# Head chunks and token sums: two chunks per store, stored by GpSimd, loaded by a gather of the feature block

## The chip, the cores and the metric

The kernel runs on one core of a Trainium2 chip. A core has five engines that work side by side, each through its own queue of instructions in order: TensorE (PE; its weight loads are shown apart as PEld), VectorE (DVE), ScalarE (ACT), GpSimd (POOL) and SyncE (SP, which here does nothing but issue transfers). Transfers between the core's memory and the chip's main memory (DMAs) are issued by SP, ACT or POOL and carried out by 16 DMA engines. The metric is the device time of one execution in microseconds (us), lower is better.

## The reference, cut to what matters

Two layers of a backbone over 1024 tokens of width 1024: a retention layer (4 heads, queries and keys of 256, values of 512, chunks of 128 tokens), a SwiGLU FFN, a short gated convolution, and a second FFN. What the change touches is the way from the heads to the o projection, and operands of the FFNs' and the convolution's last products:

```python
def retention_output(o, g, w_o):
    bsz, nh, L, dv = o.shape
    o = o * lax.rsqrt(jnp.mean(o * o, axis=-1, keepdims=True) + EPS)
    o = o.transpose(0, 2, 1, 3).reshape(bsz, L, nh * dv).astype(g.dtype)
    return (jax.nn.silu(g) * o) @ w_o
...
        hx = hx + g1 * yx
        fx = modulate(rms_norm(hx, norm_ffn[i]), sh2, sc2)
        hx = hx + g2 * swiglu(fx, ffn_w1[i], ffn_w3[i], ffn_w2[i])
```

Here `o` is each head's retention output, `g` the gate and `w_o` a matrix of 2048 by 1024. All is fp32.

## The kernel before

**Products.** Every fp32 product is made of three passes of a split type (`mm3`, L130 low part of one operand, L131 of the other, L132 both high parts). The operands come from `split`: ACT casts the high part (L125), DVE subtracts it for the low part (L126). The large projections do seven products of half matrices in place of eight, so they need sums and differences of operands: n = 1 to 7 names the product. The operands that several products share are written to main memory by whoever makes them and loaded again by the projection.

**The retention phase** (up to about 890 us) goes through the heads one after the other and, in each, through chunks in both directions. `read` (L730) multiplies queries with the state and with the chunk's values, `update` renews the state (L723 and L724 make its high and low parts on ACT and DVE). L672 (ACT) and L673 (POOL) split the values. At the end of a head, each chunk c of eight goes through `finish` (L766): DVE multiplies it by the gate that `gate` has loaded (L763, L769), PE transposes it in four pieces (L774) into one bank, ACT copies it out (L776) to a tile `og` of 128 partitions by 512, which is four feature blocks of 128 by the 128 tokens of the chunk. `store` (L780) writes it from ACT to `og_d`, whose layout is [partition, feature block, 512 tokens]: one chunk goes to four pieces of 512 bytes in each partition. Then `o_finish` runs what the chunk before has left in `o_late`: the sums over tokens that the o projection's seven products need, `first` (head 1 minus head 0, L811) and `others` (three, L816, L818 and L820, when the second head of a pair is in its second half of tokens), each stored to `os_d` in the same way. In all 24 stores to `og_d` and 32 to `os_d`, 256 KB each, by ACT.

**The o projection** follows in the same instruction streams: its first operands are made while the last head ends. `down` (L1120) runs the products in the order n = 1, 5, 6, 3, 7, 4, 2, each with eight steps of 12 matmuls; for each step it loads an operand tile from `og_d` or `os_d` (`x_loads`, L1145; a whole feature block, 512 tokens, in one piece of 2 KB in each partition), up to three ahead, and pieces of `w_o` (`w_load`, L1132), makes the sums of weights (L1159, L1161) and splits both. `load_h` (L1173) loads the residual from `in_xT`. `o_src` says which tile a step reads. The FFNs and the convolution use the same `down` with operands from `x_d`: `x_steps` makes them and `put` stores them from ACT (182 stores, L1267).

**What sets the order.** The kernel is written as steps that are queued, and a scheduler of the framework fixes the order of instructions on each engine when the program is built. Transfers that SP and ACT issue are given eight landing counters (DMAHW0 to DMAHW7 in the listings below) in turn; a transfer waits, in its engine's queue, until the one before on its counter has landed. POOL's transfers have eight counters of their own (DMASW0 to DMASW7). An engine stands still while the instruction at the head of its queue waits.

Of the kernel before, what the change touches and what calls it, by code (L numbers as in the profile page):

```python
# [17 lines left out]
P = 128  # L18
# [33 lines left out]
def hybrid_kernel(ctx: ExitStack, tc: tile.TileContext, a: dict):  # L52
    nc = tc.nc
# [14 lines left out]
    def raw():  # L68

        return up.tile([P, 1024], F32, tag="u", name="raw")  # L70
# [450 lines left out]
    og_d = spilled("og_d", HEADS, NTB, shape=(P, 4, 512))  # L521
    os_d = spilled("os_d", 4, HEADS // 2, shape=(P, 4, 512))
    x_d = spilled("x_d", 7, FT // 2)
# [47 lines left out]
    for kt, h in enumerate(ch):  # L571
        if kt % 2 == 0:
            x = unit()
# [68 lines left out]
    vs, qh, kh, sh, st, s_hl, part, loaded, gates = {}, {}, {}, {}, {}, {}, {}, {}, {}  # L642
# [123 lines left out]
    def finish(h, c):  # L766

        gt = gates[h, c]
        nc.vector.scalar_tensor_tensor(  # L769
            gt, part[h, c], ys[h][:, c : c + 1], gt, op0=ALU.mult, op1=ALU.mult  # L770
        )
        ot = bank()
        for b in range(4):
            nc.tensor.transpose(ot[:, b * P : (b + 1) * P], gt[:, b * P : (b + 1) * P], ident)  # L774
        og, put = o_place(h, c)
        nc.scalar.copy(og, ot)  # L776
        t = slice((c % 4) * P, (c % 4 + 1) * P)

        def store(dst, src):
            nc.scalar.dma_start(dst[:, :, t], src.rearrange("p (b t) -> p b t", b=4))  # L780

        if (h % 2, c // 4) != (0, 1):
            store(og_d[h][c // 4], og)
        o_finish()
        if put is not None:
            o_late.append(lambda: put(store))
        gate(h, c + G_AHEAD)


# [1 line left out]
    o_parts, o_late = {}, []  # L791
# [5 lines left out]

    def o_place(h, c):

        p, i, j, c4 = h // 2, h % 2, c // 4, c % 4  # L800
        if (i, j) == (1, 1):
            og = ttile()
        else:
            if c4 % 2 == 0:
                o_parts[p, "r"] = raw()
            og = o_parts[p, "r"][:, (c4 % 2) * 512 : (c4 % 2 + 1) * 512]
            o_parts[p, i, j, c4] = og

        def first(store):
            x11 = o_parts[p, 0, 0, c4]  # L810
            nc.vector.tensor_sub(x11, og, x11)  # L811
            store(os_d[0][p], x11)

        def others(store):
            t1, x12, x21 = (o_parts.pop((p, *k, c4)) for k in ((0, 0), (0, 1), (1, 0)))
            nc.vector.tensor_sub(t1, og, t1)  # L816
            store(os_d[1][p], t1)
            nc.vector.tensor_sub(x12, og, x12)  # L818
            store(os_d[2][p], x12)
            nc.vector.tensor_sub(x21, x21, t1)  # L820
            store(os_d[3][p], x21)

        return og, {(0, 1): first, (1, 1): others}.get((i, j))

    seq = [(None, [(0, n) for n in range(NCX)])]
# [292 lines left out]
    def down(src, nh, w, gate, residual, order, consume, then=(), last=False):  # L1120
# [15 lines left out]
        def x_loads(end, must=False):  # L1136

            while loaded[0] < min(end, len(seq)):
                m = loaded[0]
                if src(*seq[m]) is None:  # L1140
                    if not must:
                        return
                    until(lambda: src(*seq[m]) is not None)
                xl[m] = ttile()
                nc.sync.dma_start(xl[m], src(*seq[m]))  # L1145
                loaded[0] += 1

        def operands(m):
# [112 lines left out]
    def x_steps(n_pairs):  # L1261


        parts, have = {}, set()

        def put(n, pr, t):
            nc.scalar.dma_start(x_d[n - 1][pr], t)  # L1267
            have.add((n, pr))

        def take(pr, i, j, t):  # L1270
            parts[pr, i, j] = t
            if (i, j) != (0, 1):
                put({(0, 0): 1, (1, 0): 2, (1, 1): 3}[i, j], pr, t)
            if all((pr, i, j) in parts for i in range(2) for j in range(2)):
                x11, x12, x21, x22 = (parts.pop((pr, i, j)) for i in range(2) for j in range(2))

                t2, t4 = [], []

                def one():
                    nc.vector.tensor_sub(x12, x12, x11)  # L1280
                    put(5, pr, x12)
                    t2.append(ttile2())
                    nc.vector.tensor_sub(t2[0], x22, x12)
                    put(6, pr, t2[0])

                def two():
                    nc.vector.tensor_sub(x11, t2[0], x11)
                    put(7, pr, x11)
                    t4.append(ttile2())
                    nc.vector.tensor_sub(t4[0], x21, t2[0])  # L1290
                    put(4, pr, t4[0])

                hooks.extend([nothing] * (4 if pr == 0 else 0) + [one, two])

        return take, lambda n, pr: x_d[n - 1][pr] if (n, pr) in have else None
# [131 lines left out]
    def o_src(n, i):  # L1427
        p, b = i // 4, i % 4
        k, tb = S_X.get(n, (0 if n == 5 else 1, 0))
        if 2 * p + k not in o_ready:  # L1430
            return None
        src = og_d[2 * p + k][tb] if n in S_X else os_d[{5: 0, 6: 1, 7: 2, 4: 3}[n]][p]
        return src[:, b]

    fx, w_plain = {}, {}
    o_ahead, o_run = down(
# [4 lines left out]
    for i, (r, _) in enumerate(seq):  # L1441
# [8 lines left out]
        if r is not None and r[1] == steps - 1:  # L1450
            h = r[0]
# [195 lines left out]
```

## Time and profile before

| what | value |
|---|---|
| median of 3 runs | 2657.06 us (2656.66 to 2660.74) |
| the profiled execution | 2653.21 us, its span 2651.4 us |
| PE busy | 2580.5 us, 97% of the span |
| DVE busy | 1944.9 us, 73% |
| ACT busy | 1191.6 us, 45% |
| POOL busy | 124.5 us, 5% |
| mean granted PE clock | 0.989 |

The span runs from the first to the last instruction of the profiled execution; the device time holds it and what lies around it. Busy time counts arithmetic only, and not the issuing of transfers; the names ACTq and SPq stand for such issues. A row of a timeline gives its start, its length, the engine, the line of the kernel, the operation with output and inputs, its shape and, in brackets, how long the engine stood idle before it and what it had waited for. The granted clock says at which share of full speed PE was allowed to run.

### The profile page before, as it was taken

To read this page: it belongs to the slowest core of one execution; us is meant where nothing else is said; L and a number is where in the kernel's file an instruction comes from. 1 tells how busy PE (TensorE), PEld (TensorE's weight loads), DVE (VectorE), ACT (ScalarE), POOL (GpSimd) and SP (SyncE) were. 2 spreads that over 40 slices of the span, in tenths; PEclk is the share of its full clock that TensorE was granted. 3 is DMA by queue.
4 is the path that set the end of the run, shared out by engine and by line. 5 is a ranking of instruction groups with operands and counts; after the bars stand their busy time and mean duration, and the time that the engine had idled before them with its cause. 6 is when DMAs were issued, how large, how long until landed. Compare 5 with 4: busy or idle time off the path is not lost.

```text
span 2651.4 us, 32772 instructions
## 1 busy us (share of the span) xinstructions
PE 2580.5 (97%) x11448; PEld 2108.8 (80%) x11448; DVE 1944.9 (73%) x3404; ACT 1191.6 (45%) x2162; POOL 124.5 (5%) x92
## 2 busy tenths in 40 slices
PE   8999999999989799999999999999999999999998
PEld 4788888887777587888888888888777888888886
DVE  4876776767887768877776878777798666567874
ACT  4743333447866436433333446433355333334452
POOL 1100221002210000000000000000000000000000
PEclk9999999999999899999999999999999999999999
DMA  9556234763668742445546734122552233328532
GB/s 330 196 166 220 83 116 151 247 226 120 201 205 270 226 126 88 147 144 178 190 152 205 267 99 155 39 81 96 177 200 72 96 109 106 111 92 300 172 100 84
DMA packets 216069, 420.43 MB, mean 159 GB/s; under 512 B 21984, under 2 KB 51808, under 8 KB 215904
## 3 DMA queue, kind: packets, MB, share of 16 engines
q1 hardware_dynamic: 134640, 310.53, 36.9%
q10 hardware_dynamic: 81264, 107.81, 11.3%
q8 instruction: 90, 1.47, 0.2%
q14 instruction: 75, 0.61, 0.1%
HBM read 308.68 MB, written 109.58 MB: 158 GB/s over the span
## 4 chain that ended last, share of the span: by engine, by line
PE 87%; DVE 5%; DMA 4%; issue 2%; ACT 1%; ACTq 0%; POOL 0%; SPq 0%; DVEq 0%; POOLq 0%
PE ps L130 28%; PE ps L131 28%; PE ps L132 28%; DVE u L126 1%; PE ps L993 1%; DVE u L724 1%; DMA og_d<-tt 0%; DVE kh L683 0%; DMA tt<-x_d 0%; DMA raw<-in_xT 0%; DMA raw<-in_w_kc 0%; PE ps L289 0%; DMA tt<-in_cxT 0%; ACT u L125 0%; PE ps L774 0%
## 5 line engine op out<-in xcount | busy, mean ns | idle before, releaser
L130 PE MATMUL ps<-u 128*128 128x512 f32 x3472 | 1364.0, 394 | 28.8 <-DVE u L126 17.0
L131 PE MATMUL ps<-u 128*128 128x512 f32 x3472 | 1360.2, 392 | 1.2 <-DVE u L126 1.2
L132 PE MATMUL ps<-u 128*128 128x512 f32 x3472 | 1357.3, 391 | 0.0
L130 PEld LDWEIGHTS ps<-u 128*128 128x128 f32 x3472 | 655.6, 189 | 174.7 <-ACT u L125 19.9
L131 PEld LDWEIGHTS ps<-u 128*128 128x128 f32 x3472 | 656.0, 189 | 140.4 <-DVE u L126 3.7
L132 PEld LDWEIGHTS ps<-u 128*128 128x128 f32 x3472 | 655.9, 189 | 137.3 <-issue 0.5
L125 ACT CAST u<-raw 128x512 fp32r<-128x512 f32 x772 | 466.7, 620 | 536.4 <-PE ps L132 277.4
L126 DVE TENSOR_TENSOR u<-raw,u 128x512 fp32r<-128x512 f32 x772 | 535.9, 707 | 157.2 <-ACT u L125 152.1
L125 ACT CAST u<-tt 128x512 fp32r<-128x512 f32 x394 | 233.1, 619 | 235.2 <-issue 56.9
L126 DVE TENSOR_TENSOR u<-tt,u 128x512 fp32r<-128x512 f32 x394 | 264.6, 695 | 87.8 <-ACT u L125 85.6
L492 ACT COPY tt<-ps 128x512 f32<-128x512 f32 x174 | 102.2, 588 | 211.6 <-PE ps L132 202.8
L724 DVE SCALAR_TENSOR_TENSOR u<-ps,u 128x512 fp32r<-128x512 f32 x128 | 84.2, 684 | 28.1 <-ACT u L723 27.9
L505 DVE TENSOR_TENSOR tt<-tt,ps 128x512 f32<-128x512 f32 x58 | 39.7, 684 | 81.4 <-PE ps L132 81.4
L1241 DVE SCALAR_TENSOR_TENSOR t<-ps,ada,t 128x512 f32<-128x512 f32 x80 | 56.0, 746 | 54.2 <-PE ps L132 54.1
L723 ACT ACTIVATE u<-ps 128x512 fp32r<-128x512 f32 x128 | 73.2, 598 | 29.5 <-PE ps L132 27.9
L499 DVE TENSOR_TENSOR tt<-tt,ps 128x512 f32<-128x512 f32 x58 | 39.7, 684 | 48.6 <-ACT tt L492 48.6
L673 POOL TENSOR_TENSOR u<-t,u 128x512 fp32r<-128x512 f32 x40 | 55.9, 1402 | 319.4 <-ACT u L672 161.4
L203 DVE SCALAR_TENSOR_TENSOR raw<-raw,c_row 128x512 f32<-128x512 f32 x84 | 55.1, 685 | 19.6 <-DMA raw<-in_ada_t 19.5
L130 PE MATMUL ps<-u,kh 128*128 128x512 f32 x144 | 57.0, 396 | 4.7 <-POOL u L673 4.7
L961 ACT COPY tt<-ps 128x512 f32<-128x512 f32 x48 | 28.1, 587 | 63.5 <-PE ps L132 62.6
L132 PE MATMUL ps<-u,kh 128*128 128x512 f32 x144 | 56.2, 390 | 0.0
L131 PE MATMUL ps<-u,kh 128*128 128x512 f32 x144 | 56.1, 390 | 0.0
(141 smaller groups left out, 1718.5 us busy)
## 6 DMA issues: line engine op xcount, KB each, us to landing
tt<-x_d SPq DMA_DIRECT2D x182, 256.0 KB, 3.5
raw<-in_w SPq DMA_DIRECT2D x88, 512.0 KB, 4.1
x_d<-tt ACTq DMA_DIRECT2D x130, 256.0 KB, 2.8
raw<-in_w SPq DMA_DIRECT2D x88, 256.0 KB, 5.0
raw<-in_ada_t SPq DMA_DIRECT2D x42, 512.0 KB, 5.2
t<-in_ada_t SPq DMA_DIRECT2D x76, 256.0 KB, 5.4
raw<-in_w_v SPq DMA_DIRECT2D x36, 512.0 KB, 5.0
x_d<-t ACTq DMA_DIRECT2D x52, 256.0 KB, 3.8
```

What stands on the lines that cost most here:

```text
L125: nc.scalar.copy(dst_hi, src)
L126: (eng or nc.vector).tensor_sub(dst_lo, src, dst_hi.bitcast(F32))
L130: nc.tensor.matmul(ps, w_hi, x_lo, start=first, stop=False, **kw)
L131: nc.tensor.matmul(ps, w_lo, x_hi, start=False, stop=False, **kw)
L132: nc.tensor.matmul(ps, w_hi, x_hi, start=False, stop=last, **kw)
L203: nc.vector.scalar_tensor_tensor(w[e], w[e], 1.0, c_row[:, k], op0=ALU.mult, op1=ALU.mult, accum_out=sums[:, e, ct : ct + 1],)
L492: nc.scalar.copy(m[p, n], ps)
L499: nc.vector.tensor_add(t, t, banks[p, "c"])
L673: nc.gpsimd.tensor_sub(t[:, 1], v, t[:, 0].bitcast(F32))
L723: nc.scalar.activation(s[:, 0], st[d][m], AF.Copy, scale=f)
L724: nc.vector.scalar_tensor_tensor(s[:, 1], st[d][m], f, s[:, 0].bitcast(F32), op0=ALU.mult, op1=ALU.subtract,)
L1241: nc.vector.scalar_tensor_tensor(h, banks[which][c], gate[:, kt : kt + 1], h, op0=ALU.mult, op1=ALU.add)
```

## The change

The two layouts change: `og_d` and `os_d` are now read as [partition, chunk of four, feature block and token], so that a chunk of a head is one piece of 2 KB in each partition and two neighbouring chunks are one of 4 KB. The pair is stored by one transfer of 512 KB, after the second of its chunks (eight for `og_d`, sixteen for `os_d`); the second half of tokens of heads 1 and 3 is stored chunk by chunk (eight). All 32 are issued by POOL, and all of them from `o_late`, that is when the next chunk has been copied. The sums write over the pair buffers in place. The loads of the o projection (56) gather a feature block from four chunks, 512 bytes from each. Of the 182 stores of `x_d`, the 104 of n = 4 to 7 are issued by POOL and the others by ACT as before.

```diff
-        og, put = o_place(h, c)
+        og, late = o_place(h, c)
         nc.scalar.copy(og, ot)
-        t = slice((c % 4) * P, (c % 4 + 1) * P)
-
-        def store(dst, src):
-            nc.scalar.dma_start(dst[:, :, t], src.rearrange("p (b t) -> p b t", b=4))
-
-        if (h % 2, c // 4) != (0, 1):
-            store(og_d[h][c // 4], og)
         o_finish()
-        if put is not None:
-            o_late.append(lambda: put(store))
+        o_late.append(late)
         gate(h, c + G_AHEAD)
...
         p, i, j, c4 = h // 2, h % 2, c // 4, c % 4
+        e = slice((c4 % 2) * 512, (c4 % 2 + 1) * 512)
         if (i, j) == (1, 1):
             og = ttile()
         else:
             if c4 % 2 == 0:
-                o_parts[p, "r"] = raw()
-            og = o_parts[p, "r"][:, (c4 % 2) * 512 : (c4 % 2 + 1) * 512]
-            o_parts[p, i, j, c4] = og
-
-        def first(store):
-            x11 = o_parts[p, 0, 0, c4]
-            nc.vector.tensor_sub(x11, og, x11)
-            store(os_d[0][p], x11)
-
-        def others(store):
-            t1, x12, x21 = (o_parts.pop((p, *k, c4)) for k in ((0, 0), (0, 1), (1, 0)))
-            nc.vector.tensor_sub(t1, og, t1)
-            store(os_d[1][p], t1)
-            nc.vector.tensor_sub(x12, og, x12)
-            store(os_d[2][p], x12)
-            nc.vector.tensor_sub(x21, x21, t1)
-            store(os_d[3][p], x21)
-
-        return og, {(0, 1): first, (1, 1): others}.get((i, j))
+                o_parts[p, i, j, c4 // 2] = raw()
+            og = o_parts[p, i, j, c4 // 2][:, e]
+
+        def part(*k):
+            return o_parts[p, *k, c4 // 2]
+
+        def store(dst, src):
+            if c4 % 2:
+                nc.gpsimd.dma_start(dst[:, c4 - 1 : c4 + 1].rearrange("p c x -> p (c x)"), src)
+
+        def late():
+            if j == 0:
+                store(og_d[h][0], part(i, 0))
+            elif i == 0:
+                t1 = part(0, 0)
+                nc.vector.tensor_sub(t1[:, e], og, t1[:, e])
+                store(os_d[0][p], t1)
+            else:
+                nc.gpsimd.dma_start(og_d[h][1][:, c4], og)
+                t1, x12, x21 = part(0, 0), part(0, 1), part(1, 0)
+                nc.vector.tensor_sub(t1[:, e], og, t1[:, e])
+                store(os_d[1][p], t1)
+                nc.vector.tensor_sub(x12[:, e], og, x12[:, e])
+                store(os_d[2][p], x12)
+                nc.vector.tensor_sub(x21[:, e], x21[:, e], t1[:, e])
+                store(os_d[3][p], x21)
+
+        return og, late
...
                 xl[m] = ttile()
-                nc.sync.dma_start(xl[m], src(*seq[m]))
+                dst, x = xl[m], src(*seq[m])
+                if len(x.shape) == 3:
+                    dst = dst.rearrange("p (c t) -> p c t", c=4)
+                nc.sync.dma_start(dst, x)
...
         def put(n, pr, t):
-            nc.scalar.dma_start(x_d[n - 1][pr], t)
+            (nc.scalar if n < 4 else nc.gpsimd).dma_start(x_d[n - 1][pr], t)
...
-        return src[:, b]
+        return src[:, :, b * P : (b + 1) * P]
```

The scheduler then sets other orders. On ACT, at the last chunks of head 3, where the o projection's first casts are, this stood (a row is the line, the operation, output and inputs with their numbers, the shape, and in brackets what it waits for; DMAHW is a landing counter):

```order
L776 COPY tt_7823<-ps_7818 128x512 [waits PE_49]
L780 DMA os_d_1_1_226<-raw_7123 512x1x128 [waits DMAHW4_49,DVE_49]
L780 DMA og_d_3_1_222<-tt_7823 512x1x128 [waits DMAHW6_49,Activation_49]
L780 DMA os_d_2_1_228<-raw_7228 512x1x128 [waits DMAHW0_49,DVE_49]
L780 DMA os_d_3_1_230<-raw_7686 512x1x128 [waits DMAHW2_49,DVE_49]
L776 COPY tt_7838<-ps_7833 128x512 [waits PE_49]
L780 DMA os_d_1_1_226<-raw_7178 512x1x128 [waits DMAHW4_49,DVE_49]
L780 DMA og_d_3_1_222<-tt_7838 512x1x128 [waits DMAHW6_49,Activation_49]
L780 DMA os_d_2_1_228<-raw_7280 512x1x128 [waits DMAHW0_49,DVE_49]
L780 DMA os_d_3_1_230<-raw_7730 512x1x128 [waits DMAHW2_49,DVE_49]
L125 CAST u_7852<-tt_7704 128x512
L125 CAST u_7856<-raw_7351 128x512
```

and this now (the casts L125 of o operands follow on one another, and the copies L776 of the last two chunks stand among them; one of these waits for a store of POOL's):

```order
L125 CAST u_7777<-tt_7644 128x512 [waits DMAHW4_49]
L776 COPY tt_7766<-ps_7761 128x512 [waits DVE_49,PE_49]
L125 CAST u_7780<-raw_7381 128x512 [waits DMAHW2_49]
L125 CAST u_7827<-tt_7686 128x512 [waits DMAHW0_49]
L125 CAST u_7831<-raw_7335 128x512
L125 CAST u_7858<-tt_7729 128x512 [waits DMAHW4_49]
L125 CAST u_7862<-raw_7337 128x512
L125 CAST u_7882<-tt_7775 128x512 [waits DMAHW7_49]
L125 CAST u_7886<-raw_7339 128x512
L776 COPY tt_7801<-ps_7796 128x512 [waits DVE_49,PE_49]
L776 COPY tt_7816<-ps_7811 128x512 [waits DMASW6_49,PE_49]
L125 CAST u_7919<-tt_7825 128x512 [waits DMAHW7_49]
```

The stores of L780 have left ACT. On POOL, at the end of head 1, the values' low parts stood alone (`t2` are values, `u` their parts):

```order
L673 TENSOR_TENSOR u_6447<-t2_6283,u_6447 128x512 [waits DVE_49,DMAHW0_49,PE_49,Activation_49]
L673 TENSOR_TENSOR u_6497<-t2_6324,u_6497 128x512 [waits DVE_49,DMAHW2_49,PE_49,Activation_49]
L673 TENSOR_TENSOR u_6552<-t2_6366,u_6552 128x512 [waits DVE_49,DMAHW5_49,PE_49,Activation_49]
L673 TENSOR_TENSOR u_6607<-t2_6421,u_6607 128x512 [waits DMAHW1_49,PE_49,Activation_49]
L673 TENSOR_TENSOR u_6670<-t2_6450,u_6670 128x512 [waits DVE_49,DMAHW3_49,PE_49,Activation_49]
```

and now stores stand between them, one each ahead of the second and third, three each ahead of the fourth and fifth (`raw` are the pair buffers):

```order
L807 DMA og_d_1_0_217<-raw_6454 128x1024 [waits Activation_49]
L673 TENSOR_TENSOR u_6491<-t2_6320,u_6491 128x512 [waits DVE_49,DMAHW2_49,PE_49,Activation_49]
L807 DMA og_d_1_0_217<-raw_6507 128x1024 [waits Activation_49]
L673 TENSOR_TENSOR u_6545<-t2_6362,u_6545 128x512 [waits DVE_49,DMAHW5_49,PE_49,Activation_49]
L817 DMA og_d_1_1_218<-tt_6556 128x512 [waits Activation_49]
L817 DMA og_d_1_1_218<-tt_6567 128x512 [waits Activation_49]
L807 DMA os_d_1_0_225<-raw_5815 128x1024 [waits DMASW0_49,DVE_49]
L673 TENSOR_TENSOR u_6597<-t2_6417,u_6597 128x512 [waits PE_49,DMAHW1_49,Activation_49,Pool_49]
L817 DMA og_d_1_1_218<-tt_6612 128x512 [waits DMASW1_49,Activation_49]
L807 DMA os_d_2_0_227<-raw_5977 128x1024 [waits DMASW2_49,DVE_49]
L807 DMA os_d_3_0_229<-raw_6454 128x1024 [waits DMASW3_49,DVE_49]
L673 TENSOR_TENSOR u_6657<-t2_6446,u_6657 128x512 [waits DMAHW3_49,PE_49,Activation_49]
```

A low part of the values that came next on POOL now comes behind these stores and behind what they wait for, DVE's sums among it.

## The prediction

> **What bounds the kernel now.** I read the page first (engine totals), then windows of single stages, then PE's idle gaps on the timeline, the chain of waits, and last the queues behind the long gaps.
>
> ```profile
> span 2651.4 us, 32772 instructions
> PE 2580.5 (97%) x11448; PEld 2108.8 (80%) x11448; DVE 1944.9 (73%) x3404; ACT 1191.6 (45%) x2162; POOL 124.5 (5%) x92
> ```
>
> TensorE (PE) is busy for all but 70.9 us of the span, so the prize is that idle time and what the clock loses after each gap. The profiled execution took 2653.21 us, 1.8 more than its span; the median of the runs is 2657.06, 3.85 higher. I work out a difference inside the profiled execution and take it off both.
>
> Which stages are idle? The columns are the window, its length, busy time and instruction count of each engine, then the granted PE clock, the DMA share and GB/s.
>
> ```profile
> core 0: us, PE busy (x) PEld busy (x) DVE busy (x) ACT busy (x) POOL busy (x), PEclk, DMA share, GB/s
> 720.00:760.00 40.00, 32.27 (x141) 25.49 (x141) 31.75 (x50) 24.46 (x48) 7.26 (x5) 0.91 0.83 260
> 790.00:830.00 40.00, 34.51 (x155) 27.24 (x155) 30.35 (x49) 28.18 (x59) 7.45 (x5) 0.96 0.86 270
> 844.00:892.00 48.00, 32.20 (x133) 24.00 (x132) 28.76 (x54) 15.91 (x29) 0.00 (x0) 0.82 0.92 287
> 866.00:900.00 34.00, 19.16 (x54) 13.91 (x55) 21.13 (x34) 11.31 (x21) 0.00 (x0) 0.70 0.97 307
> 892.00:985.00 93.00, 93.00 (x408) 76.88 (x408) 74.39 (x124) 38.60 (x70) 0.00 (x0) 0.98 0.45 136
> 1050.00:1430.00 380.00, 380.00 (x1679) 314.63 (x1678) 293.61 (x550) 145.36 (x253) 0.00 (x0) 1.00 0.48 153
> ```
>
> The same columns for the transposes of L774 alone, which are shorter than the products (PE, PEld, clock, DMA share, GB/s):
>
> ```profile
> 720.00:760.00 40.00, 4.77 (x32) 3.68 (x32) 0.91 0.83 260
> 790.00:830.00 40.00, 4.19 (x29) 3.34 (x28) 0.96 0.86 270
> ```
>
> Where PE never idles, a matmul takes 93.00/408 = 0.228 us; this is the pace that I hold the other windows against. A transpose takes 0.44/4 = 0.11 us (chain rows below). What is lost against the pace:
>
> - 866 to 900: 34 - 54 x 0.228 = **21.7 us**
> - 720 to 760: 40 - 109 x 0.228 - 32 x 0.11 = **11.6 us**
> - 790 to 830: 40 - 126 x 0.228 - 29 x 0.11 = **8.1 us**
>
> The first is where the retention phase ends and the o projection begins, the others are the ends of heads 1 and 2. The FFN window (from 1050) loses nothing: there the change can only cost. Now the gaps; in brackets stands how long PE sat idle and who released it.
>
> ```profile
> 734.20 0.51 PE L130 MATMUL ps<-u,kh 128*128 128x512 f32 x1 [2.37 <-POOL u L673]
> 749.68 0.79 PE L130 MATMUL ps<-u 128*128 128x512 f32 x1 [3.28 <-DVE u L724]
> 802.16 0.51 PE L130 MATMUL ps<-u,kh 128*128 128x512 f32 x1 [2.38 <-POOL u L673]
> 824.17 0.63 PE L130 MATMUL ps<-u 128*128 128x512 f32 x1 [2.46 <-DVE u L724]
> 867.75 0.47 PE L130 MATMUL ps<-u 128*128 128x512 f32 x1 [2.13 <-DVE u L126]
> 883.03 0.76 PE L130 MATMUL ps<-u 128*128 128x512 f32 x1 [10.40 <-DVE u L126]
> 891.22 0.47 PE L130 MATMUL ps<-u 128*128 128x512 f32 x1 [2.62 <-ACT u L125]
> ```
>
> Of the 21.7 us, 2.13 + 10.40 + 2.62 = 15.15 are gaps; the other 6.5 are matmuls that take 0.47 us and more behind a gap, at a mean granted clock of 0.70. Who held the releasers? Pieces of the chain of waits, then of the queues of ACT and SP:
>
> ```profile
> 848.79 0.44 PE ps L774 x4
> 862.29 8.11 DMA os_d<-raw
> 870.48 5.63 DMA og_d<-tt
> 876.18 7.13 DMA og_d<-tt
> 883.76 6.00 DMA raw<-in_w_o
> ```
> ```profile
> 860.87 5.35 ACTq L780 DMA_DIRECT2D os_d<-raw  x3
> 877.52 3.98 ACTq L780 DMA_DIRECT2D os_d<-raw  x2
> 881.55 0.62 ACT L125 CAST u<-tt 128x512 fp32r<-128x512 f32 x1 [8.47 <-DMA og_d<-tt]
> 858.45 6.66 SPq L1173 DMA_DIRECT2D t<-in_xT  x4
> 873.68 10.04 SPq L1145 DMA_DIRECT2D tt<-os_d  x5
> ```
>
> The cast at 881.55 makes the operand that PE wants at 883.03. It stands in ACT's queue behind stores, and each of them is issued only when an earlier transfer has landed: landings, not casts, fill the chain from 862 to 883. SP's loads and ACT's stores are given the same eight landing counters in turn, so they also hold each other: five loads took SP 10.04 us. This is the wait that the change breaks, since POOL's transfers get counters of their own.
>
> **The change part by part.**
>
> *End of the retention phase.* The og_d and os_d stores leave ACT, and the casts then wait for their own load alone. I take the gap of 10.40 as gone. That of 2.62 too: its w_o load stood on SP behind the five os_d loads. **-13.0 us.** I keep the 2.13, which comes before the worst of the queue, and the 6.5 of slow matmuls, as some gap will be left. Bounds: -2.6 if only the last gap goes; -(21.7 - 2.1) = -19.6 if the slow stretch goes as well. What stays is traffic: 48 us x 287 GB/s = 13.8 MB between 844 and 892.
>
> *Ends of heads 1 and 2.* At head 1, again from the chain, from ACT and from POOL:
>
> ```profile
> 747.24 0.39 ACTq L780
> 747.92 0.72 ACTq L780
> 728.82 1.21 ACTq L780 DMA_DIRECT2D og_d<-raw  x2
> 732.77 1.37 POOL L673 TENSOR_TENSOR u<-t,u 128x512 fp32r<-128x512 f32 x1 [3.49 <-ACT u L672]
> 740.57 1.41 POOL L673 TENSOR_TENSOR u<-t,u 128x512 fp32r<-128x512 f32 x1 [6.42 <-ACT u L672]
> 750.38 1.38 POOL L673 TENSOR_TENSOR u<-t,u 128x512 fp32r<-128x512 f32 x1 [8.40 <-ACT u L672]
> ```
>
> Two of ACT's store issues (0.39 + 0.72) are in the chain ahead of the L723 and L724 that end the gap of 3.28, and a landing stands ahead of these. I take 2.4 of the 3.28. Another pair of issues (1.21) delays the L672 whose low part POOL makes at 732.77, before the gap of 2.37: 1.2. Head 1: -3.6. Head 2 has gaps of the same kinds, 2.38 + 2.46 = 4.84; half: -2.4. Together **-6.0 us**, bounds 0 and all four gaps, -10.5.
>
> *What it adds on POOL.* No row shows a transfer issued by POOL, so its price c has bounds: 0.6 us, an issue on ACT (1.21/2), and 4.8, the landing of such a store (row below), if POOL were held that long. I take 1.4, POOL's own L673, the nearest row on that engine.
>
> ```profile
> L673 POOL TENSOR_TENSOR u<-t,u 128x512 fp32r<-128x512 f32 x40 | 55.9, 1402 | 319.4 <-ACT u L672 161.4
> os_d<-raw ACTq DMA_DIRECT2D x32, 256.0 KB, 4.8
> tt<-os_d SPq DMA_DIRECT2D x32, 256.0 KB, 3.8
> x_d<-tt ACTq DMA_DIRECT2D x130, 256.0 KB, 2.8
> ```
>
> At head 1 POOL now has one store ahead of the second and of the third L673, and three ahead of the fourth and of the fifth; it was idle for 3.49, 6.42 and 8.40 us before the last three. Three stores fit in 6.42 up to c = 2.1, so at 1.4 they cost no time by themselves. But one of these stores waits for DVE's sum ahead of it in POOL's order, and the sum overwrites a pair buffer that must have landed first (4.8). L673 and then PE's state update wait behind it. I charge **+2.0 us**, one landing less the time that POOL spends meanwhile on the other two stores of that row of three (4.8 - 2 x 1.4); bounds 0 and 4.8.
>
> *Stores of x_d for n >= 4 on POOL, loads that gather.* 104 of 182 x_d stores leave ACT for an engine that is idle there (POOL 0.00 in the FFN window). PE is at 100% in that window with ACT busy 145 of 380 us: **0**. If the cover went, the late thing would be a load of x_d that waits for its store: 2.8 us on ACT, 4.8 as the worst on POOL, so +2 at the first product of each of the three down projections that read x_d: +6 at most. The 56 gathered loads write four pieces where they wrote one; the stores did that before, and the slower of the two kinds of row is 4.8 against 3.8, so a load costs at most 1.0 more, against 3 products of 12 x 0.228 = 2.7 us loaded ahead: **0**. The bytes are the same, and fewer stores are issued.
>
> The Trainium skill, DMA: Bandwidth & Descriptors, section "Anatomy of one DMA — SWDGE (gpsimd) path", fits 2.0 us and bytes/436e3 us for a transfer issued by GpSimd: for a pair store of 512 KB 3.2 us, an estimate from that page. No run so far shows one; by it the c of 4.8 would be out of reach and the +2.0 would be about half.
>
> **Sum:** -13.0 - 6.0 + 2.0 = -17.0. The profiled execution goes from 2653.21 to 2636.2 and the median from 2657.06 to **2640.1**.
>
> **The rivals.**
>
> *A. The transfers themselves bound the end of the phase.* The highest rate in four microseconds there, in the columns of the first windows:
>
> ```profile
> 864.00:868.00 4.00, 1.87 (x8) 1.15 (x7) 1.09 (x2) 1.62 (x3) 0.00 (x0) 1.00 1.10 376
> ```
>
> At 376 GB/s the 13.8 MB need 36.7 us of the 48: 11.3 to be had at most, less the 2.0 of new waits; the head ends, with DMA shares of 0.83 and 0.86, then give nothing: 2657.06 - 9.3 = 2647.8. For it: a DMA share of 0.92. Against it: residual and weight loads in that traffic aren't wanted by 892.
>
> *B. Only ACT's issue time is saved.* Landings come as late as before, the loads wait for them, and the end of the phase keeps its 21.7 us; the head ends give 6.0 - 2.0: 2653.1. For it: the chain is of landings. Against it: the landings are serialized by the issues, and the memory is only at 287 of 376 GB/s. The Trainium skill, same page, section "Issuing engines are not separate DMA queues", says that issuing from several engines saves only the sequencer's time to issue; taken strictly that is this rival. The rows of ACT's queue speak against it here, as the issues wait, and no run yet decides it.
>
> *C. The waits move, and nothing is won.* Where the sums of two heads are made, at the ends of heads 1 and 3, DVE waits for a whole landing of a pair store, 4.8 each, and at the end of the phase the wait for the pairs takes the place of the gap of 10.40, so that only the last gap goes: 2 x 4.8 - 2.6 - 6.0 = +1.0, 2658.1. For it: the pair buffers are written over in place. Against it: DVE was busy for only 28.76 of the 48 us.
>
> *D. Slower: a store holds POOL until it has landed.* At c = 4.8 the place is the ends of heads 1 and 2, and what it holds is L673, which PE's state update waits for. At head 1: 3 x 4.8 - 6.42 = 8.0, 3 x 4.8 - 8.40 = 6.0, and 2 x (4.8 - 3.49) = 2.6. At head 2 four single stores between L673s: 4 x 1.3 = 5.2. In all +21.8, against -13.0 at the end of the phase: +8.8, 2665.9. It grows by 12 us per us of c and turns the balance from c = 4.1. For it: POOL works in order. Against it: neither ACT nor SP is held by its own transfers' landing when a counter is free.
>
> **How the numbers follow.** The forecast has 0.58, A 0.14, B 0.09, C 0.09, D 0.10. A change within 0.2% (5.3 us) can't be told from none here. The forecast and A are faster by more: 0.72; B (-4.0) and C are within: 0.18; D is slower: 0.10. The forecast's own range comes from its terms, with the end of the phase at -5 less or -6 more and +-4 for heads and POOL: 2629 to 2649. With all bounds on the good side, -19.6 - 10.5 gives 2627; so I take 2626. Above, it takes in A, B and C: 2658, which leaves D out, 0.10, and a little of the forecast.
>
> **What would show it.** On PE after 866 the gap of 10.40 is gone or under 3, and 866 to 900 holds over 90 products where it held 54. In ACT's queue no store stands between 857 and 885. On POOL each issue takes under 2.1 us, and the first matmul behind L673 waits no longer than 2.4. The FFN window stays at 100% PE. I am wrong if the casts at L125 still wait over 5 us for og_d or os_d loads (A or B), if DVE's sums wait for landings (C), or if the L673 of heads 1 and 2 begin late behind stores (D).

## The result, and the profile after

The changed kernel takes 2632.81 us (median of 4 runs, 2630.79 to 2633.11), the kernel before 2656.86 (2656.11 to 2660.74) beside it. The ratio is 0.9905, with a 95% interval of 0.9888 to 0.9922: 24 us faster. In the two profiled executions the difference is 2653.21 - 2632.68 = 20.5 us. The one of before was 3.65 us below the median of its runs, that of after is at its median; this is most of what separates 20.5 from 24.

The page after, and the windows that were read before (the same columns: window, length, PE, PEld, DVE, ACT, POOL, clock, DMA share, GB/s):

```profile
span 2630.9 us, 32927 instructions
PE 2571.0 (98%) x11448; PEld 2103.4 (80%) x11448; DVE 1943.5 (74%) x3404; ACT 1196.7 (45%) x2162; POOL 197.5 (8%) x228
```
```profile
720.00:760.00 40.00, 34.20 (x156) 27.27 (x157) 33.28 (x52) 26.51 (x53) 13.40 (x17) 0.96 0.75 272
785.00:825.00 40.00, 34.21 (x156) 27.40 (x157) 30.95 (x52) 29.84 (x59) 9.18 (x9) 0.96 0.89 290
844.00:892.00 48.00, 41.98 (x188) 33.51 (x187) 37.42 (x62) 21.02 (x39) 6.51 (x12) 0.93 1.01 324
866.00:900.00 34.00, 28.02 (x116) 22.39 (x114) 27.79 (x47) 13.25 (x25) 0.24 (x1) 0.90 0.93 284
1050.00:1430.00 380.00, 379.14 (x1673) 313.68 (x1672) 281.84 (x529) 145.36 (x249) 21.69 (x40) 1.00 0.51 169
```

Between 866 and 900 us PE does 116 products where it did 54; against the pace of 0.228 us it loses 34 - 116 x 0.228 = 7.6 us where it lost 21.7. The FFN window is all but unchanged (379.14 us of 380 where it was 380.00).

PE's gaps on the timeline, and behind the largest of them the chain of waits and SP's queue:

```profile
732.27 1.09 PE L774 MATMUL ps<-ident,tt 128*128 128x128 f32 x4 [2.75 <-DVE tt L769]
740.57 0.51 PE L130 MATMUL ps<-u,kh 128*128 128x512 f32 x1 [1.07 <-POOL u L673]
797.67 0.63 PE L774 MATMUL ps<-ident,tt 128*128 128x128 f32 x4 [2.75 <-DVE tt L769]
819.84 0.50 PE L130 MATMUL ps<-u 128*128 128x512 f32 x1 [1.78 <-DVE u L724]
878.16 2.07 PE L130 MATMUL ps<-u 128*128 128x512 f32 x4 [5.98 <-ACT u L125]
```
```profile
853.14 5.69 DMA tt<-os_d
858.90 16.58 DMA tt<-os_d
875.51 0.63 ACT u L125
```
```profile
858.90 11.91 SPq L1151 DMA_DIRECT2D tt<-os_d  x4
```

The three gaps of 2.13, 10.40 and 2.62 at the start of the o projection have become one of 5.98. Between 857 and 885 us no store stands in ACT's queue any more. What ACT waits for now is a load of os_d that landed 16.58 us after its issue.

Where the time came from is read by the same instructions in both traces, since PE's order is nearly the same. Two such anchors (a line's instructions with the start of the first and the last; the line of the output's sum has another number after the change):

```profile
L1241 DVE SCALAR_TENSOR_TENSOR t<-ps,ada,t x80: 732/745/752, 910.5 to 2636.3; 128x512 f32<-128x512 f32 x80
```
```profile
L1247 DVE SCALAR_TENSOR_TENSOR t<-ps,ada,t x80: 734/746/752, 891.8 to 2615.6; 128x512 f32<-128x512 f32 x80
```

| from one anchor to the next | before | after | difference |
|---|---|---|---|
| start to head 1's first transposes (L774) | 721.51 | 720.61 | -0.9 |
| to head 2's first transposes (789.45, 785.99) | 67.94 | 65.38 | -2.6 |
| to head 3's first transposes (847.91, 843.56) | 58.46 | 57.57 | -0.9 |
| to the o projection's first such sum (910.5, 891.8) | 62.6 | 48.2 | -14.4 |
| to the last such sum (2636.3, 2615.6) | 1725.8 | 1723.8 | -2.0 |

The -0.9 of the first row lies ahead of everything that the change touches at a head's end. In the later profiles this anchor falls anywhere between 720.6 and 725.2; so much can a single execution differ before it reaches the change, and single profiles are compared from this anchor on.

### The profile page after: what moved, and what is told of

Read it like the earlier page. It is cut to its first block, busy times and chain, and to the rows that moved or that the text cites. A ratio compares the mean times of both kernels' runs of the same rounds, so it can differ in the third digit from the quotient of the medians.

```text
span 2630.9 us, 32927 instructions
## 1 busy us (share of the span) xinstructions
PE 2571.0 (98%) x11448; PEld 2103.4 (80%) x11448; DVE 1943.5 (74%) x3404; ACT 1196.7 (45%) x2162; POOL 197.5 (8%) x228
## 4 chain that ended last, share of the span: by engine, by line
PE 87%; DVE 5%; DMA 4%; issue 1%; ACT 1%; SPq 0%; ACTq 0%; DVEq 0%
PE ps L130 29%; PE ps L131 29%; PE ps L132 28%; DVE u L126 1%; DMA tt<-os_d 1%; DMA raw<-in_w_kc 1%; DVE u L724 1%; PE ps L996 1%; DMA tt<-g_d 0%; DVE kh L683 0%; PE ps L774 0%; ACT u L125 0%; DMA tt<-in_cxT 0%; DMA raw<-in_xT 0%; PE ps L263 0%
## 5 line engine op out<-in xcount | busy, mean ns | idle before, releaser
L125 ACT CAST u<-raw 128x512 fp32r<-128x512 f32 x772 | 467.6, 620 | 493.1 <-PE ps L132 321.7
L125 ACT CAST u<-tt 128x512 fp32r<-128x512 f32 x394 | 233.0, 619 | 238.4 <-issue 60.0
L492 ACT COPY tt<-ps 128x512 f32<-128x512 f32 x174 | 102.4, 589 | 243.2 <-PE ps L132 238.0
L1273 POOL DMA_DIRECT2D x_d<-tt x52 | 28.2, 542 | 1450.8 <-DVE tt L1286 1434.2
L724 DVE SCALAR_TENSOR_TENSOR u<-ps,u 128x512 fp32r<-128x512 f32 x128 | 84.8, 683 | 19.9 <-ACT u L723 19.7
L673 POOL TENSOR_TENSOR u<-t,u 128x512 fp32r<-128x512 f32 x40 | 55.0, 1378 | 277.8 <-DMA t<-v_d 139.8
```

The lines of the kernel that those rows point to most:

```text
L125: nc.scalar.copy(dst_hi, src)
L492: nc.scalar.copy(m[p, n], ps)
L673: nc.gpsimd.tensor_sub(t[:, 1], v, t[:, 0].bitcast(F32))
L724: nc.vector.scalar_tensor_tensor(s[:, 1], st[d][m], f, s[:, 0].bitcast(F32), op0=ALU.mult, op1=ALU.subtract,)
```

## The experiments

Ratios are against runs of the kernel before on the same chip in the same sitting, with their 95% intervals.

**Only the x_d stores on POOL.** The kernel before with

```diff
-            nc.scalar.dma_start(x_d[n - 1][pr], t)
+            (nc.scalar if n < 4 else nc.gpsimd).dma_start(x_d[n - 1][pr], t)
```

> The kernel before with one edit: the 104 stores of x_d for n = 4 to 7 are issued by POOL. Theory (the FFN stages run at 100% PE and an ACT queue with room to spare, so these stores were never on the path): within 2 us of the kernel before, ratio 0.999 to 1.001, and the gap of 10.40 us before the o projection's products unchanged. Rival (the x_d stores held ACT or the landing counters in the FFNs and gave a share of the gain): 3 to 8 us faster, 2649 to 2654.

Measured: 2658.5 us beside 2657.7, ratio 1.0004 (0.9995 to 1.0013), and the old stall stands:

```profile
886.14 0.77 PE L130 MATMUL ps<-u 128*128 128x512 f32 x1 [11.64 <-DVE u L126]
```

The 104 stores of `x_d`, out of the 136 that POOL issues after the change, are worth nothing that shows, as their stage said: PE is at 100% there.

**Only the heads' stores on POOL.** The changed kernel with that line put back:

```diff
-            (nc.scalar if n < 4 else nc.gpsimd).dma_start(x_d[n - 1][pr], t)
+            nc.scalar.dma_start(x_d[n - 1][pr], t)
```

> The changed kernel with the x_d stores left on ACT: only the head chunks and token sums are stored by POOL, in the new layout. Theory: all of the gain but at most 1.5 us is here: 2632 to 2636, and the matmul after the end of the retention phase waits about 6 us as in the changed kernel. Rival (x_d gives a share): 2637 to 2645.

Measured: 2633.36 us, ratio 0.9909 (0.9893 to 0.9924), with a gap like that of the changed kernel (5.98):

```profile
877.03 2.07 PE L130 MATMUL ps<-u 128*128 128x512 f32 x4 [5.68 <-ACT u L125]
```

The whole gain is in what the change does to the heads' stores and the loads that read them.

**The same, issued by ACT.** From the run above, the engine alone goes back:

```diff
-                nc.gpsimd.dma_start(dst[:, c4 - 1 : c4 + 1].rearrange("p c x -> p (c x)"), src)
+                nc.scalar.dma_start(dst[:, c4 - 1 : c4 + 1].rearrange("p c x -> p (c x)"), src)
...
-                nc.gpsimd.dma_start(og_d[h][1][:, c4], og)
+                nc.scalar.dma_start(og_d[h][1][:, c4], og)
```

> As the run with x_d on ACT, but the pair stores and the single ones of og_d are issued by ACT in place of POOL: layout, pairing, late stores and gathered loads are those of the change, only the issuing engine goes back. Theory (the casts stood behind stores in ACT's queue that waited for landings shared with SP): most of the gain goes, 2645 to 2655, with casts at L125 again waiting 5 us or more behind stores and SP's issues stretched. Rival (fewer and larger stores, or their later place, made the gain, whoever issues them): 2632 to 2638.

Measured: 2641.21 us, ratio 0.9941 (0.9929 to 0.9954), between the two. ACT's queue again has arithmetic that stands behind stores:

```profile
862.74 5.41 ACTq L807 DMA_DIRECT2D os_d<-raw  x3
868.25 0.58 ACT L776 COPY tt<-ps 128x512 f32<-128x512 f32 x1 [6.46 <-DMA os_d<-raw]
874.36 4.58 ACTq L807 DMA_DIRECT2D os_d<-raw  x3
878.99 0.62 ACT L125 CAST u<-tt 128x512 fp32r<-128x512 f32 x1 [6.81 <-DMA os_d<-raw]
```

By the ratios, whose intervals lie apart, the engine alone is worth some 8 us (0.9941 against 0.9909); some 16 are had with ACT as issuer, by the layout, the pairs or the later place. My expectation that most of the gain goes with the engine was wrong in size.

**The old layout, issued by POOL.** The kernel before with

```diff
-            nc.scalar.dma_start(dst[:, :, t], src.rearrange("p (b t) -> p b t", b=4))
+            nc.gpsimd.dma_start(dst[:, :, t], src.rearrange("p (b t) -> p b t", b=4))
```

> The kernel before with one edit: the 56 stores of og_d and os_d at L780 are issued by POOL, in the old layout with 512-byte pieces, one chunk each, at the old places, and the loads as before. Theory (the issuing engine's queue decides): most of the gain is kept, 2633 to 2642; POOL issues cost under 0.8 us each, 56 of them, so L673 is not delayed by more than 2 us at a head's end. Rival (pairs of 4 KB pieces make it): 2648 to 2657.

Measured: 2631.18 us, ratio 0.9902 (0.9885 to 0.9918): all of the gain of the change, with one word of it. The four residual loads stand where they stood in the kernel before, ahead of the os_d loads (L1173 from 857.7 us). With POOL as issuer the new layout, the pairs and the gathered loads add nothing that the intervals show. The longest gap of PE at the end of the phase is now this:

```profile
878.49 2.08 PE L130 MATMUL ps<-u 128*128 128x512 f32 x4 [2.61 <-ACT u L125]
```

The 512-byte pieces cost POOL more (the three durations are least, median and greatest, in ns), which the time does not show:

```profile
L780 POOL DMA_DIRECT2D os_d<-raw x32: 709/817/1470, 686.1 to 872.1; - x32
```
```profile
L807 POOL DMA_DIRECT2D os_d<-raw x16: 533/539/573, 684.2 to 865.7; - x16
```

The first row is of this run, the second of the changed kernel.

**The old layout, issued by SP.** The same line with `nc.sync`. ACT is freed, but the stores use SP's landing counters and its queue.

> The kernel before with one edit: the 56 stores at L780 are issued by SP. ACT is freed as by the change, but the stores share SP's landing counters and its queue with the loads. Theory (what hurt was that casts stood behind stores in ACT's queue): a good part of the gain is kept, 2636 to 2648, less than with POOL since loads now stand behind stores that wait for DVE's sums. Rival (the shared landing counters hurt, whoever issues): no gain or slower, 2653 to 2665.

Measured: 2632.05 us, ratio 0.991 (0.9896 to 0.9923): all of the gain again, though loads and stores still share one set of eight counters. SP's stores stand in SP's queue, between its loads, and ACT's casts do not stand behind them; the longest gap of PE at the end of the phase is 4.47 us (last row):

```profile
864.08 2.60 SPq L780 DMA_DIRECT2D os_d<-raw  x3
872.98 8.00 SPq L1145 DMA_DIRECT2D tt<-os_d  x9
881.33 1.76 SPq L1173 DMA_DIRECT2D t<-in_xT  x4
867.89 0.76 PE L130 MATMUL ps<-u 128*128 128x512 f32 x1 [4.47 <-DVE u L126]
```

With this order the scheduler also puts four residual loads at 881 us, behind the os_d loads; in the kernel before, four stood at 858 (6.66 us). So this run differs from the kernel before in more than the issuer, and I don't read more from it than that a gain of this size is possible without counters of the stores' own.

**Single rows on ACT.** From the pairs on ACT, each chunk by itself, as late as there:

```diff
-            if c4 % 2:
-                nc.scalar.dma_start(dst[:, c4 - 1 : c4 + 1].rearrange("p c x -> p (c x)"), src)
+            nc.scalar.dma_start(dst[:, c4], src[:, e])
```

> As the run with pair stores on ACT, but each chunk is stored by itself (2 KB pieces in each partition), late as there: 56 stores of 256 KB in place of 32, x_d on ACT. Theory (with ACT as issuer the number of stores that wait for a landing counter in ACT's queue decides): most of the 16 us that pairing gave on ACT go, 2648 to 2656. Rival (the row layout or the later place gave them): 2638 to 2644.

Measured: 2642.06 us, ratio 0.9948 (0.9934 to 0.9962), as with pairs (0.9941). The number of stores does not decide: pairing is worth nothing on ACT either. Waits for landings are still in ACT's queue:

```profile
860.79 4.18 ACTq L806 DMA_DIRECT2D os_d<-raw  x3
865.01 0.59 ACT L776 COPY tt<-ps 128x512 f32<-128x512 f32 x1 [7.80 <-DMA os_d<-raw]
871.01 0.76 PE L130 MATMUL ps<-u 128*128 128x512 f32 x1 [9.19 <-DVE u L126]
```

The long gap is still 9.19 us (last row). By the same anchors this run gains 5.2 us on the kernel before between head 1's and head 2's first transposes, 2.1 to head 3's, and 6.1 to the o projection's first sum; so with ACT as issuer about half of the gain lies at the ends of heads 1 and 2.

**Single rows on ACT, og_d stored at once.** From the run above, the og_d store goes back to its old place, right after the copy:

```diff
         nc.scalar.copy(og, ot)
+        early()
         o_finish()
...
```

(`early` is the store of og_d, taken out of `late`.)

> As the run with single rows on ACT (2642), but og_d is stored at once after its copy, as in the kernel before, and only the sums later. Theory (the row layout, whose issue takes ACT 0.33 us in place of 0.52, and the shorter queue it makes, gave 15 us even on ACT): 2640 to 2645. Rival (the later place of the og_d stores gave it): 2650 to 2657.

Measured: 2648.64 us, ratio 0.9967 (0.9956 to 0.9979), between what the two theories said. So of the gain that is had with ACT as issuer, the row layout (with its gathered loads) gives 0.33% (8.8 us); the later place gives another 0.19% by the medians (0.9948 against 0.9967, 5 us), though the two intervals overlap. The layout shortens what an issue takes on ACT, from 0.52 us (the og_d rows of before) to 0.33 us here, and the later place puts casts and copies that PE waits for ahead of the stores; that these are the reasons is argued and not shown. The gaps remain (9.79 and 3.42 us of PE), and so do the waits in ACT's queue:

```profile
869.10 3.72 ACTq L807 DMA_DIRECT2D os_d<-raw  x2
872.86 0.59 ACT L776 COPY tt<-ps 128x512 f32<-128x512 f32 x1 [6.95 <-DMA og_d<-tt]
```

**What is left: residual loads later.** Now the gap of 5.98 of the changed kernel:

```diff
-                if i == 0:
-                    if n in (1, 5, 6, 7):
-                        load_h({1: 1, 5: 5, 6: 6, 7: 4}[n])
+                if n in (1, 5, 6, 7) and i == (nh // 2 if n == 5 else 0):
+                    load_h({1: 1, 5: 5, 6: 6, 7: 4}[n])
+                if i == 0:
```

> The changed kernel with the four residual loads for n = 5 issued four steps later (at that product's fifth step in place of its first), so that 1 MB less stands ahead of the first os_d loads in SP's queue. Theory (what is left of the stall, 5.98 us before a product of n = 5, is an os_d load that needed 16.6 us to land because the memory moved 346 GB/s of other things): the gap falls under 3 us and the time by 3 to 6, to 2627 to 2630. Rival (the load waits for a counter or for the pair store, not for bytes): unchanged, 2631 to 2634.

Measured: 2635.52 us, ratio 0.9922 (0.991 to 0.9935), no gain. But it did not test what it was meant to: the scheduler issued the four loads where they had stood before.

```profile
855.64 2.77 SPq L1179 DMA_DIRECT2D t<-in_xT  x4
859.29 12.10 SPq L1151 DMA_DIRECT2D tt<-os_d  x4
878.11 2.07 PE L130 MATMUL ps<-u 128*128 128x512 f32 x4 [5.55 <-ACT u L125]
```

Whether those loads are what delays os_d stays open.

**Pairs split by four.** From the run with only the heads' stores on POOL:

```diff
-                nc.gpsimd.dma_start(dst[:, c4 - 1 : c4 + 1].rearrange("p c x -> p (c x)"), src)
+                for r in range(4):
+                    q = slice(r * 32, r * 32 + 32)
+                    nc.gpsimd.dma_start(
+                        dst[q, c4 - 1 : c4 + 1].rearrange("p c x -> p (c x)"), src[q]
+                    )
```

> As the run with only the heads' stores on POOL, but each pair store is issued as four transfers of 32 partitions each, so POOL issues 104 for the heads in place of 32, with the same bytes in the same pieces. It puts four times the price of a pair store on POOL ahead of L673. Theory (POOL's idle time hides up to about 2.1 us ahead of each L673, and an issue costs 0.54): 4 x 0.5 = 2.2 us per pair, at the limit of the cover: 0 to 5 us slower than the run it is made from, 2633 to 2639. Rival (issues on POOL are on the path at the heads' ends, as in the case that I named D): 8 us slower or more, 2641 to 2655, with L673 beginning over 4 us later behind stores.

Measured: 2624.6 us (2623.59 to 2628.18), ratio 0.9884 (0.9869 to 0.9899). Neither theory had it faster than the run that it is made from (0.9909), and it has the best median of all runs; its interval overlaps that of the changed kernel, and that of the run it is made from, a little. An issue costs 0.49 us, so 2.0 us for a pair. The gap of 5.98 is gone:

```profile
859.96 0.47 PE L130 MATMUL ps<-u 128*128 128x512 f32 x1 [1.39 <-DVE u L126]
869.17 1.20 PE L130 MATMUL ps<-u 128*128 128x512 f32 x4 [0.18 <-ACT u L125]
```

That gave a new theory. POOL waits for a landing when its eight counters are taken; smaller transfers mean that fewer bytes of its stores can be outstanding (issued and not yet landed), and the os_d loads have less to land behind. Such waits are in this trace: nine of os_d stores behind os_d stores, 7.4 us in all. In the changed kernel no store of og_d or os_d waits on POOL for a landing, so nothing holds them back there. Three runs tested the theory.

**Pieces split by two, pairs split by two, single rows, all on POOL.** The first is the old layout on POOL with two transfers of 64 partitions (`dst[q, :, t]`, `src[q]`) for each store; the second is the split above with `range(2)` and 64 partitions; the third is

```diff
-            if c4 % 2:
-                nc.gpsimd.dma_start(dst[:, c4 - 1 : c4 + 1].rearrange("p c x -> p (c x)"), src)
+            nc.gpsimd.dma_start(dst[:, c4], src[:, e])
```

> The kernel before with its stores at L780 issued by POOL in the old layout, each as two transfers of 64 partitions (128 KB). POOL has eight landing counters, so at most 8 x 128 KB = 1 MB of its stores can be outstanding, as in the run that split pairs by four; with whole pieces it was 2 MB, with pairs 4 MB. Theory (what is left of the stall comes from POOL's outstanding stores, behind which the os_d loads land late: 16.6 us at worst with 4 MB, 13.3 with 2 MB, 9.4 with 1 MB): 2622 to 2628, the longest landing of os_d under 10.5 us and no gap over 2 us after the retention phase. Rival (the new layout's rows, or something else in that split kernel): as with whole pieces on POOL, 2629 to 2634.

> As the run with the heads' pair stores on POOL (x_d on ACT), each pair in two transfers of 64 partitions, 256 KB: at most 2 MB outstanding, pieces of 4 KB as before. Theory (outstanding bytes): between the whole pairs and the split by four, 2626 to 2631, longest landing of os_d 11 to 14 us, gap 2 to 4 us. Rival (size of the pieces decides how loads and stores share the queues): as whole pairs, 2632 to 2636, landing 16.

> As the run with the heads' stores on POOL (x_d on ACT), but each chunk stored by itself: 256 KB in pieces of 2 KB, at most 2 MB outstanding. Theory (outstanding bytes): as with pairs split in two, 2626 to 2631. Rival (size of the pieces): better than pairs split in two by 3 us or more, since their pieces stay at 4 KB.

Measured, in this order: 2634.39 us, ratio 0.9913 (0.9896 to 0.9929); 2637.99, 0.9927 (0.9912 to 0.9942); 2638.66, 0.9932 (0.9917 to 0.9947). In time the theory fell: none of them is faster than the changed kernel. For the landings at the place that it speaks of, it held:

| kernel | bound of the eight counters on POOL's stores | most outstanding in the trace | longest landing among os_d's stores and loads | gaps of PE over 0.5 us from 860 on | PE busy, 844 to 892 |
|---|---|---|---|---|---|
| changed kernel, pairs | 8 x 512 KB, single chunks 256 | 3.0 MB | 16.6 us | 5.98 | 41.98 |
| pieces on POOL | 8 x 256 KB | 2.0 | 13.3 | 1.11, 2.61 | 44.17 |
| pairs split by two | 8 x 256 KB | 2.0 | 12.9 | 1.60, 2.63 | 43.67 |
| rows on POOL | 8 x 256 KB | 2.0 | 13.5 | 0.66, 4.95 | 42.27 |
| pairs split by four | 8 x 128 KB, single chunks 256 | 1.25 | 9.4 | 1.39 | 46.39 |
| pieces split by two | 8 x 128 KB | 1.0 | 8.8 | none | 47.65 |

The gap of 1.39 is at 859.96. The landing shrinks with the bytes, whatever the pieces' size (4 KB, 2 KB or 512 bytes). It is counted from the issue, and a wait ahead of the issue is not in it: the kernel before has a longest landing of 9.1 us and the largest gaps of all. The gaps follow the bytes less closely than the landings do: with the same 2.0 MB they add up to 3.7, 4.2 and 5.6 us. One thing beside the bytes differs there: where the loads are gathered, single issues on SP took long, the longest for os_d 7.75 us in the changed kernel, 6.70 with rows on POOL, 2.69 with pairs split by two and 1.74 with pairs split by four, but 0.86 and 1.10 in the two kernels with the old layout. Whether that widens a gap was not tested. The row of the changed kernel:

```profile
L1151 SPq DMA_DIRECT2D tt<-os_d x32: 517/525/7747, 844.2 to 961.1; - x32
```

The last kernel of the table has the fullest window of all (first row):

```profile
844.00:892.00 48.00, 47.65 (x221) 37.81 (x220) 43.24 (x80) 20.80 (x41) 23.78 (x40) 1.00 0.96 337
745.65 1.09 PE L774 MATMUL ps<-ident,tt 128*128 128x128 f32 x4 [5.04 <-DVE tt L769]
735.68 2.47 POOL L782 DMA_DIRECT2D og_d<-tt  x4
737.93 3.86 POOL L782 DMA_DIRECT2D os_d<-raw  x6
```

and gives part of it back at the end of head 1, as the second row shows: with 112 issues of 0.6 us for the heads POOL has long rows of them (the last two rows), and the transposes of the last chunks wait for 5.04 us. The chain of waits ahead of that gap, as the profile infers it, goes through POOL's issues and the landing of a store, then 2.54 us for which it shows no wait, then one of DVE's sums and the product that the transposes wait for (L769, from 744.84 us):

```profile
735.68 1.02 POOL og_d L782 x2
736.82 1.33 POOL og_d L782 x2
738.50 2.37 DMA os_d<-raw
741.02 2.54 issue
743.56 0.68 DVE raw L820
```

From head 1's first transposes to head 2's it needs 791.53 - 724.74 = 66.8 us where the changed kernel needs 65.4 and the whole pieces on POOL 62.6 (786.45 - 723.88). Over the whole stretch to the last sum its profile is still the shorter, 1890.5 us against 1895.0 for the changed kernel, so its median, 1.6 us above that of the changed kernel, is not explained by this gap alone.

For the pairs split by two and the single rows no such loss is in the profile. From head 1's first transposes to the last sum they take 1891.1 and 1897.1 us, the changed kernel 1895.0; why their medians are 5 to 6 us above its own is not settled. The profiled execution of each (2633.6 and 2638.19 us) is the fastest of its four, so it shows little of what the others lost. Nor does the long gap account for the 8 us of the pairs split by four. Their profile shows 1885.6 us over the same stretch, 9.4 less than the changed kernel: 1.3 less to head 2's first transposes, 4.3 from there to head 3's, 2.4 to the o projection's first sum and 1.3 behind it. So under a third of it lies where the gap was.

## Why the prediction was right, and where it was not

It said 2640, in a range of 2626 to 2658; the time is 2632.8. The sum was -17.0 in the profiled execution, which measured -20.5. The direction, the place and the total held; that the total came so near is partly luck, as terms that were off by several us made up for each other.

- **End of the phase, -13.0: measured -14.4**, to the o projection's first sum (62.6 to 48.2). The place and the size held, the working did not. Of the gaps of 15.15 us, 5.98 are left: 9.2 gained and not 13.0. The slow matmuls, which I kept at 6.5, are down to 7.6 - 5.98 = 1.6: 4.9 more, which is what hides the gap that stayed. The granted clock in that window goes with the gaps: 0.70 with three of them, 0.90 with this one, and 1.00 with the pairs split by four and the pieces split by two, where from 866 us on no gap is over 0.5 us.
- **The reason given, that stores and loads hold each other through shared landing counters and that POOL's own counters break this, is not borne out.** The run with SP as issuer keeps loads and stores on one set of counters and has the whole gain, though with later residual loads. And the rows of before, in the prediction, show for the most part stores that hold stores: the store that starts at 862.29 lands at 870.40, the next one in the chain starts at 870.48 and lands at 876.11, and the next at 876.18. All three are ACT's own; the listing of ACT's order has its last eight stores on four counters in turn (DMAHW4, 6, 0, 2). What the runs show of the cost: ACT's arithmetic stood in order behind stores that waited (8.47 us before the cast at 881.55; 6.46 and 6.81 us again with pairs on ACT), and each of the two other issuers gave the whole gain. What ACT would do with eight counters of its own was not run.
- **Ends of heads, -6.0, with the new waits +2.0: measured -2.6 - 0.9 = -3.5**, near the -4.0. The gap behind L673 at head 1 fell from 2.37 to 1.07, that behind L724 from 3.28 to 0.42, and one of 2.75 behind L769 came, twice, so that the -2.4 for head 2 was too much. The first of these follows a gate load in the chain of waits, not a sum that waits for a store:

```profile
724.54 6.58 DMA tt<-g_d
731.15 0.98 DVE tt L769
```

- **POOL's price c: 0.54 us, taken as 1.4.** It is just under my lower bound of 0.6. This closed D. C's waits of 4.8 at DVE's sums are not there: none of the sums waits for a landing in the changed kernel's trace. (`first`, L811, which stands ahead of the prediction as head 1 minus head 0, is the second half of tokens less the first of heads 0 and 2; the sums at the ends of heads 1 and 3 are those of `others`.) The other estimate of a landing, 3.2 us for a pair store, was too low: the pairs took 5.4 us (og_d) and 6.5 us (os_d) in the median. By 3.2 the +2.0 would have been 3.2 - 2.8 = 0.4, and not the half that the prediction says.
- **x_d stores and gathered loads, 0:** the x_d stores alone gave a ratio of 1.0004. The gathered loads take SP longer to issue (below) and cost no time that a run shows, since the old layout on POOL is no faster than the change.
- **A came true in part.** The sign that I had named for A or B, a cast that waits over 5 us for a load, is there: 14.5 us, at 376 GB/s between 860 and 876. But it costs one gap of 5.98, the time is 15 us below A's 2647.8, and the bytes are not yet a floor: the split by four fits 4.4 us more work of PE into the same window at the same 324 GB/s.

```profile
875.51 0.62 ACT L125 CAST u<-tt 128x512 fp32r<-128x512 f32 x1 [14.54 <-DMA tt<-os_d]
860.00:876.00 16.00, 12.14 (x50) 8.85 (x48) 9.95 (x16) 1.46 (x3) 2.69 (x5) 0.97 1.06 376
```
```profile
844.00:892.00 48.00, 46.39 (x210) 36.98 (x210) 40.99 (x68) 20.52 (x39) 15.89 (x32) 1.00 0.98 324
```

The first fence is of the changed kernel, the second of the split by four.

- **B fell.** The rule of the Trainium skill, DMA: Bandwidth & Descriptors, "Issuing engines are not separate DMA queues", that issuing from several engines saves only the sequencer's time to issue, would have left the end of the phase as it was. The measurement decides otherwise: the same 56 stores, moved from ACT to POOL, are worth 0.98%, 26 us. By the rows of ACT's queue, what is lost there is not only the 0.5 us of an issue but the wait ahead of it, with the casts behind.

## What to carry to other kernels

Look at what stands behind a store in its engine's queue: a store that waits for a landing or a sum holds all arithmetic behind it, and an engine with nothing urgent behind (POOL or SP here) can issue it in its place. Change the issuer alone first; here a new layout, pairing and 104 more moved stores came with it and added nothing that could be measured. When the issuer is free to run ahead, look next at how many bytes of its stores are outstanding, since the loads here took the longer to land the more there were, and at how many issues stand ahead of its own arithmetic. Neither of these two was turned into time in a way that held in every run.

## What the runs showed of the hardware that was not expected

The price of an issue depended on the shape and differed by engine. On ACT a store of one chunk in four pieces for each partition took 0.52 us, in whole rows 0.33, also as a pair of 512 KB. The rows of ACT and SP follow, first of the kernel before, then of the pairs on ACT, again of before, and of the changed kernel (least, median, greatest in ns):

```profile
L780 ACTq DMA_DIRECT2D og_d<-raw x16: 520/521/602, 666.4 to 855.9; - x16
```
```profile
L807 ACTq DMA_DIRECT2D os_d<-raw x16: 326/326/1012, 688.0 to 878.6; - x16
```
```profile
L1145 SPq DMA_DIRECT2D tt<-og_d x24: 319/320/486, 808.6 to 1009.6; - x24
```
```profile
L1151 SPq DMA_DIRECT2D tt<-og_d x24: 517/522/912, 801.8 to 991.0; - x24
```

On POOL a pair of os_d took 0.54 in the median, a quarter of its partitions 0.49, and a chunk in 512-byte pieces 0.82, at the least 0.71. On SP a load took 0.32 us as one piece for each partition and 0.52 as a gather of four.

The longest landing among os_d's transfers grew with the most bytes of POOL's stores that were outstanding in the trace: 8.8 us with 1.0 MB, 9.4 with 1.25, 12.9 to 13.5 with 2.0, 16.6 with 3.0, at rates between 307 and 339 GB/s in the 48 us window. That the bytes outstanding are the cause rests on these six kernels; nothing else was held still in all of them.
